# Letting the products of two heads take turns in the scan of an RWKV-7 layer

## The chip, the cores and the metric

The kernel runs on one core of a Trainium2 chip. The metric is the device time of one execution in microseconds (us). The kernel before takes 3988.88 us, the median of three runs (3987.24 to 3991.28). Products of matrices run on TensorE (PE in the profile; its loads of the stationary operand are listed as PEld), everything elementwise on VectorE (DVE), ScalarE (ACT) and GpSimd (POOL); SyncE (SP) and others start DMAs.

## The reference, cut to what matters

One encoder layer for 1024 tokens of 1024 numbers: a combined projection, a branch with forgetting attention, a branch with RWKV-7 time mixing (8 heads of 64), a gated merge, and a block of product-key experts. The change lies in the RWKV-7 branch, whose reference is a loop over the tokens:

```python
def frame_step(state, inp):
    r_t, w_t, k_t, v_t, kk_t, a_t = inp
    sa = jnp.einsum('bhij,bhj->bhi', state, -kk_t)
    state = (state * w_t[:, :, None, :] + sa[..., None] * (kk_t * a_t)[:, :, None, :]
             + v_t[..., None] * k_t[:, :, None, :])
    return state, jnp.einsum('bhij,bhj->bhi', state, r_t)
```

Each head carries a state of 64 x 64; every token decays it, corrects it and reads one row of output from it. All is float32.

## The kernel before, in words

`body` takes the tokens in two halves of 512. A half goes through `fox` (attention), `rwkv_half`, `merge_half` and `queries`; after the second half comes a long phase for the experts (`dense_block`), from about 2070 us to the end, in which PE is busy nearly all the time.

`rwkv_half` treats the eight heads in four groups `ct` of two heads `e`. The two heads of a group share the 128 partitions: `rows[0]` is partitions 0 to 63, `rows[1]` 64 to 127. `unit(ct)` computes one group in chunks of 64 tokens; a half has NC = 8 chunks `c`. It first prepares, for all chunks at once, the matrices that each chunk needs: masked products `M`, transposed operands `BK` and `AV`, a triangular inverse built up in six levels (`Tm`, `Vm`, products of 64 x 64 blocks in PSUM tiles named `s`), and from them `At` (a tile named `Tm`), which carries a head's state over one chunk, and `Q` (a tile named `x`), which reads the outputs.

Then comes the scan (lines 1020 to 1034), the only part that goes chunk by chunk. A step has eight products, four for each head:

- BK: `pss[r] = BK[:, e, c] x AV[:, e, c]` (line 1026), over all 128 partitions with 64 output rows: the profile writes its place on the array as 128*64, and its names as `s<-AV,BK`.
- At: `pss[r] += At[r, c] x sigma[r]` (line 1027), over the head's own 64 partitions, 64*64, `s<-sigma,Tm`. `sigma` is the state.
- M: `py[r, c] = AV x M` (line 1031), 128*64, `s<-M,AV`.
- Q: `py[r, c] += sigma x Q` (line 1032), 64*64, `s<-x,sigma`.

Head 0 writes partitions 0 to 63 of the PSUM tile, head 1 partitions 64 to 127. Between At and M a copy (line 1028) brings `pss` back to SBUF as the next state; DVE makes it in even steps, ACT in odd ones, and there are two places for the state, taken in turn. The next step's At waits for that copy; M and Q of the same step still read the old state. In the profile every float32 product is two PE instructions (x2).

All products go through the helper `mm` (line 262), so they all carry line 263. `mm` also ticks a background (`g.B`): the work for the experts (top-k, gathers of expert rows by POOL, reduces by DVE, line 1403) is issued piece by piece between the products, by an account of estimated product times, and stands between the kernel's own instructions on DVE and POOL. It has something to do only from the second half on, once the first half's scores are known. After each step `wait(WT[7])` lets a filler issue about 1 us of gate projections (`pj` products of 512 columns, lines 324 to 334), as long as there are some left for this group: in the first three groups they fill the places after the first and the second step of a scan, in the fourth those after the first four steps. The steps behind them are bare. PE takes its instructions in the order in which they are written (`manual_schedule`).

Of the kernel before, what the change touches and what calls it, by code (L numbers as in the profile page):

```python
# [261 lines left out]
def mm(g, o, l, r, start, stop_):  # L262
    g.pe.matmul(o, l, r, start=start, stop=stop_)  # L263
    n = 1
    for d in r.shape[1:]:
        n *= d
    us = max(n, 256) / 2400.0 if r.dtype == F32R else max(4 * n, 256) / 2400.0
    g.V.tick(us)
    if not g.V.busy:
        g.B.tick(us)  # L270
# [470 lines left out]
def rwkv_half(g, hf, X, kt):  # L741
# [3 lines left out]
    rows = (slice(0, 64), slice(64, 128))  # L745
# [8 lines left out]
    with ExitStack() as fx:  # L754
# [164 lines left out]
        def unit(ct):  # L919
# [3 lines left out]
            def wait(us):  # L923
                F.fill(WAIT * us)
# [64 lines left out]
            for u in range(0, NC, 8):  # L989
# [3 lines left out]
                for c in range(n8):  # L993
                    for e in range(2):
                        r = rows[e]
                        mm(g, pw[r, c, :], Vm[r, u + c, :], AV[r, e:3:2 - e, u + c, :], True, True)
                act.copy(W_[:, us], pw[:, :, 0:64])
                for e in range(2):
                    r = rows[e]
# [3 lines left out]
            for e, c in items:  # L1003
                r = rows[e]
# [9 lines left out]
            for e, c in items:  # L1014
                r = rows[e]
# [5 lines left out]
            for c in range(NC):  # L1021
                par = c % 2
                pss = psS.tile([128, 64], F32, name="s")
                for e in range(2):
                    r = rows[e]
                    mm(g, pss[r, :], BK[:, e, c, :], AV[:, e, c, :], True, False)
                    mm(g, pss[r, :], At[r, c, :], g.sigma[r, ct, par, :], False, True)
                (act.copy if c % 2 or SM & 64 else dve.tensor_copy)(g.sigma[:, ct, 1 - par, :], pss)
                for e in range(2):
                    r = rows[e]  # L1030
                    mm(g, py[r, c, :], AV[:, e, c, :], M[:, e, c, 0:64], True, False)
                    mm(g, py[r, c, :], g.sigma[r, ct, par, :], Q[r, c, :], False, True)
                wait(WT[7])
            act.copy(yr[:, ct, :], fl(py))
# [13 lines left out]
        for ct in range(4):  # L1048
            F.add(bonus(ct))
            if ct < 3:  # L1050
                F.add(elem(ct + 1), f"e{ct + 1}")
            gates(NG[1 + ct])
            unit(ct)
            if ct < 3:
                F.drain(f"e{ct + 1}")
# [785 lines left out]
```

## Time and profile before

| | |
|---|---|
| median of three runs | 3988.88 us |
| profiled execution | 3954.7 us |
| its span | 3952.9 us |
| PE busy | 3367.2 us (85%), 20656 instructions |
| DVE busy | 2310.8 us (58%) |
| POOL busy | 2341.8 us (59%) |
| ACT busy | 1243.7 us (31%) |
| mean clock granted to TensorE | 0.897 of full speed |

The span is that of one execution, taken by the hardware profiler. A row of a timeline gives start, duration, engine, line, operation, output<-inputs by the program's names, for a product its place on the array (rows*columns) and the moving operand's shape, and in brackets the idle time before it with what ended it. PE is pipelined and the ends of its instructions are modelled: the pace is read from the starts. A table of stretches gives each engine's busy time, and the clock that TensorE was granted as a share of full speed.

### The profile page before, as it was taken

What the parts mean: (1) busy time and instruction counts of PE and PEld (TensorE: products, weight loads), DVE (VectorE), ACT (ScalarE), POOL (GpSimd) and SP (SyncE); (2) the same over time, 40 slices, a digit from 0 to 9 for tenths busy, and PEclk for the clock granted to TensorE, in tenths of its full rate; (3) what the DMA queues carried; (4) which work ended last, traced back from release to release, by engine and by line L of the source; (5) the groups of instructions that cost most, each with busy time, mean ns of one, the idle gap of its engine ahead of it and who ended that gap; (6) DMA issues with size and microseconds to landing.
All of it is one profiled execution on the core that took longest, in us unless ns stands there. A gap on an engine that the chain in (4) does not pass through costs nothing. (4 is left out here: it accounts for less than half of the span.)

```text
span 3952.9 us, 55417 instructions
## 1 busy us (share of the span) xinstructions
PE 3367.2 (85%) x20656; PEld 2429.7 (61%) x20656; DVE 2310.8 (58%) x4773; ACT 1243.7 (31%) x2522; POOL 2341.8 (59%) x1848
## 2 busy tenths in 40 slices
PE   7999999989987877877837676699998899999998
PEld 5577676775555655656713333477776677776676
DVE  3133423448889887899637576366665576733334
ACT  3342212333333111122214343233333333333333
POOL 2031114435666546667647667688887788777872
PEclk9898898998988777888968778799999899999999
DMA  4121114447777666877768789999998999999993
GB/s 134 43 91 36 36 63 138 168 150 243 259 256 260 213 213 223 292 252 262 278 250 269 263 289 301 322 362 367 375 349 319 374 377 387 376 367 406 403 407 128
DMA packets 376575, 1018.03 MB, mean 258 GB/s; under 512 B 108273, under 2 KB 124913, under 8 KB 376049
## 3 DMA queue, kind: packets, MB, share of 16 engines
q0 software_dynamic: 184320, 671.17, 46.5%
q1 hardware_dynamic: 179872, 322.54, 23.9%
q10 hardware_dynamic: 12112, 20.78, 1.4%
q8 instruction: 162, 2.65, 0.3%
q14 instruction: 109, 0.88, 0.1%
HBM read 960.03 MB, written 54.33 MB: 257 GB/s over the span
## 5 line engine op out<-in xcount | busy, mean ns | idle before, releaser
L1398 POOL DMA_INDIRECT g<-u,eidx x640 | 779.0, 1217 | 436.5 <-DVE hh L1403 154.6
L1403 DVE CUSTOM_DVE_ANT_0 g<-g,ext 128x1024 f32<-128x1024 f32 x640 | 879.5, 1382 | 230.3 <-DMA g<-u,eidx 228.7
L281 POOL TENSOR_TENSOR wl<-wraw,wh 128x1024 fp32r<-128x1024 f32 x131 | 322.9, 2465 | 562.4 <-ACT wh L280 513.1
L1675 POOL DMA_INDIRECT vr<-v,ve x454 | 488.6, 1076 | 130.3 <-issue 104.1
L263 PE MATMUL pg<-vr,win 128*32 128x512 f32 x1816 | 307.8, 645 | 115.6 <-DMA vr<-v,ve 115.3
L263 PE MATMUL b<-xh,uh 128*128 128x384 f32 x1024 | 353.7, 345 | 52.2 <-DVE C L1561 29.6
L263 PE MATMUL b<-xh,ul 128*128 128x384 f32 x1024 | 357.4, 349 | 19.1 <-POOL ul L281 19.1
L263 PE MATMUL b<-xl,uh 128*128 128x384 f32 x1024 | 351.9, 344 | 0.0
L263 PE MATMUL v<-vl,ch 128*128 128x512 f32 x768 | 310.1, 404 | 22.7 <-POOL vl L281 22.6
L263 PE MATMUL pj<-xh,wh 128*128 128x512 f32 x624 | 292.0, 468 | 22.3 <-DVE ql L546 8.5
L280 ACT CAST wh<-wraw 128x1024 fp32r<-128x1024 f32 x150 | 157.2, 1048 | 486.3 <-PE pj L263 264.3
L263 PE MATMUL v<-vh,cl 128*128 128x512 f32 x768 | 305.3, 398 | 0.0
L263 PE MATMUL v<-vh,ch 128*128 128x512 f32 x768 | 304.7, 397 | 0.0
L280 ACT CAST uh<-uraw 128x512 fp32r<-128x512 f32 x256 | 158.7, 620 | 399.4 <-PE b L263 359.0
L263 PE MATMUL pj<-xh,wl 128*128 128x512 f32 x624 | 262.0, 420 | 6.4 <-POOL wl L281 3.7
L263 PE MATMUL pj<-xl,wh 128*128 128x512 f32 x624 | 263.9, 423 | 1.9 <-DVE xl L281 1.9
L1675 POOL DMA_INDIRECT C<-v,ve x186 | 196.6, 1057 | 105.3 <-issue 39.4
L263 PEld LDWEIGHTS b<-xh,uh 128*128 128x128 f32 x1024 | 196.7, 192 | 66.5 <-DVE C L1561 34.3
L263 PEld LDWEIGHTS b<-xh,ul 128*128 128x128 f32 x1024 | 196.6, 192 | 56.6 <-issue 32.7
L281 POOL TENSOR_TENSOR ul<-uraw,uh 128x512 fp32r<-128x512 f32 x128 | 170.6, 1333 | 92.8 <-ACT uh L280 66.7
L281 DVE TENSOR_TENSOR vl<-vraw,vh 128x512 fp32r<-128x512 f32 x128 | 122.8, 960 | 171.4 <-ACT vh L280 164.7
L263 PEld LDWEIGHTS pg<-vr,win 128*32 128x32 f32 x1816 | 52.3, 112 | 275.2 <-DMA vr<-v,ve 191.4
(352 smaller groups left out, 6897.9 us busy)
## 6 DMA issues: line engine op xcount, KB each, us to landing
wraw<-w SPq DMA_DIRECT2D x150, 512.0 KB, 3.5
uraw<-ut SPq DMA_DIRECT2D x128, 512.0 KB, 6.9
vraw<-vt SPq DMA_DIRECT2D x128, 512.0 KB, 6.7
cd<-S SPq DMA_DIRECT2D x30, 512.0 KB, 15.6
C<-cd SPq DMA_DIRECT2D x80, 192.0 KB, 6.1
g<-u,eidx POOLq DMA_INDIRECT x640, 6.1
gtd<-tmp ACTq DMA_DIRECT2D x32, 256.0 KB, 3.1
g<-gtd SPq DMA_DIRECT2D x32, 256.0 KB, 3.3
```

The source lines that it names most:

```text
L263: g.pe.matmul(o, l, r, start=start, stop=stop_)
L280: g.act.copy(hi, src)
L281: (lo_eng or g.dve).tensor_sub(lo, src, hi.bitcast(F32))
L1398: pool.indirect_dma_start(out=gg, out_offset=None, in_=A["u"], in_offset=bass.IndirectOffsetOnAxis(ap=idx[:, s_:s_ + 1], axis=0))
L1403: dve.tensor_tensor_reduce(out=gg, in0=gg, in1=xt, scale=1.0, scalar=0.0, op0=OP.mult, op1=OP.add, accum_out=hh[:, k:k + 1])
L1675: g.pool.indirect_dma_start(out=place, out_offset=None, in_=g.A["v"], in_offset=bass.IndirectOffsetOnAxis(ap=self.meta[i][1][:, t:t + 1], ...
```

## The change

The two loops over the heads, each with two products in its body, become four loops with one product each. What is multiplied, added and copied stays the same; only the order of the eight products of a step differs. The wait of the first At product for the state now stands behind both BK products.

```diff
             for c in range(NC):
                 par = c % 2
                 pss = psS.tile([128, 64], F32, name="s")
-                for e in range(2):
-                    r = rows[e]
+
+                for e, r in enumerate(rows):
                     mm(g, pss[r, :], BK[:, e, c, :], AV[:, e, c, :], True, False)
+                for r in rows:
                     mm(g, pss[r, :], At[r, c, :], g.sigma[r, ct, par, :], False, True)
                 (act.copy if c % 2 or SM & 64 else dve.tensor_copy)(g.sigma[:, ct, 1 - par, :], pss)
-                for e in range(2):
-                    r = rows[e]
+                for e, r in enumerate(rows):
                     mm(g, py[r, c, :], AV[:, e, c, :], M[:, e, c, 0:64], True, False)
+                for r in rows:
                     mm(g, py[r, c, :], g.sigma[r, ct, par, :], Q[r, c, :], False, True)
                 wait(WT[7])
```

PE's order at the start of the first scan, before the change: the first step, between the projection that precedes it and the one that fills behind it. The tile s_2412 is `pss` of this step, s_2411 is `py`, Tm_2380 is `At`, x_2406 is `Q`.

```order
L263 MATMUL pj_2323<-xh_84,wl_2218 128x512
L263 MATMUL s_2412<-AV_1788,BK_1787 64x64
L263 MATMUL s_2412<-sigma_138,Tm_2380 64x64
L263 MATMUL s_2412<-AV_1788,BK_1787 64x64
L263 MATMUL s_2412<-sigma_138,Tm_2380 64x64
L263 MATMUL s_2411<-M_1786,AV_1788 64x64
L263 MATMUL s_2411<-x_2406,sigma_138 64x64
L263 MATMUL s_2411<-M_1786,AV_1788 64x64
L263 MATMUL s_2411<-x_2406,sigma_138 64x64
L263 MATMUL pj_2323<-xh_84,wh_2217 128x512
```

The same place after the change (x2 here: the product of head 0, then that of head 1).

```order
L263 MATMUL pj_2323<-xh_84,wl_2218 128x512
L263 MATMUL s_2412<-AV_1788,BK_1787 64x64 x2
L263 MATMUL s_2412<-sigma_138,Tm_2380 64x64 x2
L263 MATMUL s_2411<-M_1786,AV_1788 64x64 x2
L263 MATMUL s_2411<-x_2406,sigma_138 64x64 x2
L263 MATMUL pj_2323<-xh_84,wh_2217 128x512
```

Each kind of product now stands twice in a row, once for each head, and the filling projection stands where it stood. Further on in the same scan, where no projections stand between the steps, before the change:

```order
L263 MATMUL s_2441<-AV_1788,BK_1787 64x64
L263 MATMUL s_2441<-sigma_138,Tm_2380 64x64
L263 MATMUL s_2441<-AV_1788,BK_1787 64x64
L263 MATMUL s_2441<-sigma_138,Tm_2380 64x64
L263 MATMUL s_2411<-M_1786,AV_1788 64x64
L263 MATMUL s_2411<-x_2406,sigma_138 64x64
L263 MATMUL s_2411<-M_1786,AV_1788 64x64
L263 MATMUL s_2411<-x_2406,sigma_138 64x64
L263 MATMUL s_2454<-AV_1788,BK_1787 64x64
```

And after it:

```order
L263 MATMUL s_2441<-AV_1788,BK_1787 64x64 x2
L263 MATMUL s_2441<-sigma_138,Tm_2380 64x64 x2
L263 MATMUL s_2411<-M_1786,AV_1788 64x64 x2
L263 MATMUL s_2411<-x_2406,sigma_138 64x64 x2
L263 MATMUL s_2454<-AV_1788,BK_1787 64x64 x2
```

The last Q product of a step is followed at once by the next step's two BK products, and the copy of the state has those, M and Q to run beside. On DVE, ACT, POOL and SP no instruction changes its place.

## The prediction

> **What bounds the kernel now.** I read the page first (TensorE, PE in the rows, is busy for 85% of the span), then the stretches of the eight scans, then the timeline inside one of them. The profiled execution took 3954.7 us, its span and 1.8 us around it; the three timed runs have a median of 3988.88 us. I work out a saving on the profiled execution and take it from that median. A measurement of this kernel tells about 0.2%, 8 us, from no change.
>
> The stretches of the eight scans (two halves of four groups), from the first product of a scan to the end of its last step. Columns: stretch, its us, then busy us and instructions of PE, PEld, DVE, ACT, POOL, then the granted clock, DMA share and GB/s.
>
> ```profile
> 344.19:367.16 22.97, 22.97 (x138) 16.32 (x137) 1.41 (x5) 2.39 (x6) 2.34 (x1) 0.76 0.11 36
> 426.87:450.28 23.41, 23.41 (x139) 16.60 (x138) 1.41 (x5) 2.39 (x6) 2.34 (x1) 0.74 0.10 34
> 509.47:533.23 23.76, 23.76 (x139) 16.85 (x138) 1.41 (x5) 2.39 (x6) 2.34 (x1) 0.72 0.10 34
> 587.68:611.28 23.60, 23.60 (x148) 16.64 (x147) 2.52 (x6) 2.39 (x6) 0.58 (x1) 0.87 0.33 112
> 1314.81:1345.01 30.20, 27.70 (x140) 19.17 (x139) 14.29 (x53) 2.39 (x6) 12.76 (x11) 0.62 0.60 202
> 1425.15:1457.80 32.65, 28.29 (x138) 19.61 (x137) 18.71 (x45) 4.45 (x8) 14.71 (x13) 0.59 0.63 206
> 1541.02:1575.23 34.21, 28.28 (x140) 19.62 (x139) 17.03 (x44) 2.39 (x6) 16.07 (x12) 0.59 0.64 214
> 1653.02:1679.59 26.57, 25.12 (x148) 17.51 (x147) 18.02 (x54) 2.39 (x6) 15.38 (x13) 0.82 0.84 287
> sum 217.37, PE 203.13 PEld 142.32 DVE 74.80 ACT 21.18 POOL 66.54; mean PE 25.39 PEld 17.79 DVE 9.35 ACT 2.65 POOL 8.32
> ```
>
> The scans take 217 us, 5.5% of the span, and in the first half nothing but PE works in them: DVE is busy 1.4 us of 23. The clock granted is 0.59 to 0.87 there. Now the inside of one scan, in which one step of the loop over c has no projection work between; each row is one product (two instructions, x2).
>
> ```profile
> 352.84 0.33 PE L263 MATMUL s<-AV,BK 128*64 128x64 f32 x2
> 353.10 0.32 PE L263 MATMUL s<-sigma,Tm 64*64 64x64 f32 x2
> 353.36 0.33 PE L263 MATMUL s<-AV,BK 128*64 128x64 f32 x2
> 353.61 0.33 PE L263 MATMUL s<-sigma,Tm 64*64 64x64 f32 x2
> 353.87 0.33 PE L263 MATMUL s<-M,AV 128*64 128x64 f32 x2
> 354.03 0.21 ACT L1028 COPY sigma<-s 128x64 f32<-128x64 f32 x1 [1.78 <-PE s L263]
> ...
> 354.89 0.33 PE L263 MATMUL s<-AV,BK 128*64 128x64 f32 x2
> ...
> 357.48 0.47 PE L263 MATMUL s<-AV,BK 128*64 128x64 f32 x2
> ...
> 360.71 0.47 PE L263 MATMUL s<-AV,BK 128*64 128x64 f32 x2
> ```
>
> A product starts every 0.26 us, whatever stands beside it, and a step of eight takes 354.89 - 352.84 = 2.05 us; later in the same scan, 360.71 - 357.48 = 3.23 us, the same step at the halved clock. The product itself cannot need 0.26 us, as other places show, with the same element type and both heads' partition halves taking turns:
>
> ```profile
> 341.29 1.15 PE L263 MATMUL s<-BK,x 64*64 64x64 f32 x32
> 342.27 1.10 PE L263 MATMUL s<-M,x 64*64 64x64 f32 x32
> 343.30 0.50 PE L263 MATMUL pj<-xh,wh 128*128 128x512 f32 x1
> 343.63 0.39 PE L263 MATMUL pj<-xl,wh 128*128 128x512 f32 x1
> 343.86 0.40 PE L263 MATMUL pj<-xh,wl 128*128 128x512 f32 x1
> 344.19 0.33 PE L263 MATMUL s<-AV,BK 128*64 128x64 f32 x2
> ...
> 2593.68 1.92 PE L263 MATMUL pg<-vr,win 128*32 128x512 f32 x16
> 2595.54 0.45 PE L263 MATMUL b<-xh,ul 128*128 128x384 f32 x1
> ```
>
> Sixteen 64*64 products start within 342.27 - 341.29 = 0.98 us: 0.06 us each, a quarter of the scan's 0.26. What differs is that those sixteen all have one shape, 64 rows by 64 columns of the array, while in the scan each product has another shape than the one before it (128*64, 64*64, 128*64, ...). It is not only that neighbours share a place: the second and third rows of the scan step lie on different columns (head 0's 64*64 corner, then head 1's 128*64 half), and are as far apart as the rest. The Trainium skill says so too ("TensorEngine Tiling (Array Packing)", Key Properties): a change of the tiling mode, not merely of the tile, drains TensorE; by that rule the scan drains eight times a step, and the trace agrees, 0.26 against 0.06 us.
>
> **The change, part by part.** It makes a step BK, BK, At, At, M, M, Q, Q: four changes of shape instead of eight. Nothing is added or removed, and on DVE, ACT, POOL and SP every instruction stands where it stood; the first 64*64 product's wait for sigma moves behind one more product.
>
> *One step.* Each pair now has one shape on two places. What the second product of a pair costs is bounded by 0.06 us (an alternating one, above) and by nearly nothing, if it runs wholly beside the first, as a pair of the sixteen does; so a pair takes 0.26 to 0.32 us. For the 128*64 pair no row exists, since all 128 rows of the array serve both; the nearest is pg, four column strips of 128*32 fed by different data: 16 instructions of 512 columns in 2595.54 - 2593.68 = 1.86 us, where 16 in line at the 0.23 us between two pj rows would take 3.7. Column strips do run side by side, so I take 0.26 for both kinds, and 0.51 (no overlap) as the far end for the 128*64 pair. A step then takes 4 x 0.26 = 1.04 us instead of 2.05.
>
> *Does sigma's chain take over?* In the step shown, the copy starts 354.03 - 353.61 = 0.42 us after the second At product starts and takes 0.21. With both At products starting together, sigma is there 0.63 us after them, and they are due again after 1.04: 0.4 us to spare. M, Q and the next BK (3 x 0.26 = 0.78 us) cover the copy. If that cover went, a step would be some 0.65 us anyway, so the chain does not bind.
>
> *First half.* PE is never idle in these four scans. A projection step between two steps (three pj with its entry) takes 344.19 - 343.30 = 0.89 us, a second one behind it 0.70. The first three scans hold three (0.89 + 1.59 = 2.5 us), the fourth six in four places (5.0). So after the change: 3 x (8.3 + 2.5) + 8.3 + 5.0 = 45.7 us, if the clock stays up; before, 22.97 + 23.41 + 23.76 + 23.60 = 93.7. Saved 48 us, 20 of it from steps at the halved clock.
>
> *The clock.* It was halved after some 5 us of bare steps; a bare stretch of six will last 6.2 us with twice the products in the time, so the clock either holds or drops near its end. Dropping costs about 1 us a scan; holding also frees what follows:
>
> ```profile
> 367.16 2.08 PE L263 MATMUL pm<-arv,bk 64*128 64x128 f32 x16
> ...
> 371.89 0.63 PE L263 MATMUL pj<-xh,wl 128*128 128x512 f32 x1
> 372.32 0.63 PE L263 MATMUL pj<-xh,wh 128*128 128x512 f32 x1
> ...
> 375.71 1.16 PE L263 MATMUL pm<-arv,bk 64*128 64x128 f32 x16
> ```
>
> The first pm after the scan takes 2.08 us instead of 1.16, and pj come every 0.43 instead of 0.23 us: some 2.5 us behind each of four scans, 10 in all. Between -4 and +10 I take +4.
>
> *Second half.* Here DVE carries the experts' reduces and the top-k, and outside the scans PE waits for it. What can be gained is the time in which DVE waits for PE:
>
> ```profile
> DVE sigma L1028 <- PE s L263: 47.4, 11, 7.1
> DVE g L1403 <- DMA g<-u,eidx: 10.7, 15, 2.5
> DVE M L937 <- PE pm L263: 9.8, 3, 3.6
> ```
>
> (waits of DVE from 1310 to 1680 us: us in total, times, longest). And DVE between two of its copies of sigma, the second bare pair of the fifth scan:
>
> ```profile
> 1333.82 0.23 DVE L1028 COPY sigma<-s 128x64 f32<-128x64 f32 x1 [3.09 <-PE s L263]
> ...
> 1334.48 1.21 DVE L1403 CUSTOM_DVE_ANT_0 g<-g,ext 128x1024 f32<-128x1024 f32 x1
> 1335.62 0.08 DVE L1403 DVE_READ_ACCUMULATOR2_ANT hh<- 128x1 f32 x1
> 1340.27 0.23 DVE L1028 COPY sigma<-s 128x64 f32<-128x64 f32 x1 [4.57 <-PE s L263]
> ```
>
> DVE works 1335.70 - 1333.82 = 1.9 us and then waits 4.57. Two steps will take 2.1 us, so the work just fits and some 0.3 us of waiting is left. The wait before the first bare copy (7.1 us, behind a filled step at low clock) shrinks only by about 2. Left over I estimate 5 us for each of three scans and 2 for the last, with 3 at pm: 20 of 47.4 + 9.8 = 57. That frees 37, and DVE, the slower engine around these scans, hands it on; gathers that now come late may take 3 of it back: 34 us, between 0 and all 57.
>
> *Sum.* 48 + 4 + 34 = 86 us: profiled 3954.7 - 86 = 3869, and the median 3988.88 - 86 = **3903 us**. What comes later moves up by it: the order on every engine is the same, and the last phase is a chain of PE.
>
> **Rivals.**
>
> 1. *DVE swallows the second half.* For it: DVE's 1.9 us between copies against 2.1 us; a gather that lands late eats that. Against: only 10.7 us of DVE waits for gathers now, longest 2.5. Saved 48 + 3 = 51: 3938 us.
> 2. *128*64 pairs do not overlap.* No row has this shape in turns; pg speaks against. A step is 2 x 0.26 + 4 x 0.26 = 1.56 us, half the saving, 24 + 18 = 42: 3947 us.
> 3. *64*64 pairs do not overlap,* as both heads write one PSUM tile from different row halves. Only the 128*64 pairs gain: 42 us again, 3947. The sixteen products at 0.06 us do just that (both halves of one tile) and speak against it. This is the Trainium skill's rule against the change ("TensorEngine Tiling (Array Packing)", Gotcha 1: PSUM Pressure): different row tiles cannot access one PSUM bank at the same time; by these rows the trace does not bear it out.
> 4. *No change:* each product drains by itself, with its accumulation, and pairs keep 0.26 each: 3989 us. The alternating rows are single products, not accumulating ones; that is all that speaks for it.
> 5. *Slower:* in the second half a copy of sigma stands behind a reduce whose gather has lost its lead, and PE waits for it. The price of one:
>
> ```profile
> L1398 POOL DMA_INDIRECT g<-u,eidx x640 | 779.0, 1217 | 436.5 <-DVE hh L1403 154.6
> L1403 DVE CUSTOM_DVE_ANT_0 g<-g,ext 128x1024 f32<-128x1024 f32 x640 | 879.5, 1382 | 230.3 <-DMA g<-u,eidx 228.7
> ...
> g<-u,eidx POOLq DMA_INDIRECT x640, 6.1
> ```
>
> Issue 1.2, landing 6.1, reduce 1.4: 8.7 us, 16 times, 139 us. The four scans last 30.20 + 32.65 + 34.21 + 26.57 = 123.6 us now, 14 of it with PE idle (PE is busy 109.4); at the new pace they would last 46 + 14 + 139 = 199, 75 more, less the first half's 52: 23 slower, 4012 us. It decides from (52 + 64) / 16 = 7.2 us a copy; the gathers are issued three reduces ahead, so I hold it unlikely.
>
> **Chances.** Forecast 0.68, rival 1 0.14, rival 2 0.08, rival 3 0.04, rival 4 0.03, rival 5 0.03. The forecast's own range goes from 48 + 10 + 57 = 115 us saved (the clock holds, DVE waits for nothing in the second half), 3874, to 40 - 4 + 18 = 54 saved (pairs of 0.32, which cost 32 steps 0.24 us each; the clock drops; half of the second half's gain), 3935. Eight in ten need most of that and rival 1: 3876 to 3942. Faster by over 0.2%: 0.68 + 0.14 + 0.08 + 0.04 = 0.94; within 0.2%: 0.03; slower: 0.03.
>
> **What would show it.** In the profile after: equal products in pairs, a bare step of 1.04 us at clock 1.00 (1.56 means that one kind does not overlap, 2.05 neither); first-half scans of 10.8 us; copies of sigma with DVE waiting under 1 us before them in the second half, the row DVE sigma <- PE s near 15 instead of 47; the waits for g<-u no longer than now. The prediction is wrong if bare steps stay above 1.5 us, or if the first half shrinks by 48 us and the second not at all.

## The result, and the profile after

The changed kernel takes 3880.14 us, the median of six runs (3873.97 to 3887.82), beside 3985.46 us of before (the median of six runs, three of them those above): 105 us less, a ratio of 0.9741 with a 95% interval from 0.9723 to 0.9759. It was forecast at 3903 us, with a range from 3876 to 3942; the time lies inside, near the fast end.

The page's first line, and the stretches of the eight scans after the change (columns as in the prediction):

```profile
span 3878.1 us, 55417 instructions
```

```profile
342.25:353.16 10.91, 10.91 (x138) 7.82 (x137) 1.42 (x5) 2.39 (x6) 2.35 (x1) 1.00 0.22 75
410.18:421.09 10.91, 10.91 (x138) 7.81 (x137) 1.42 (x5) 2.39 (x6) 2.35 (x1) 1.00 0.20 74
478.08:488.99 10.91, 10.91 (x138) 7.81 (x137) 1.42 (x5) 2.39 (x6) 2.35 (x1) 1.00 0.20 73
541.71:555.10 13.39, 13.39 (x147) 9.35 (x146) 2.63 (x6) 2.39 (x6) 0.58 (x1) 1.00 0.47 156
1271.26:1289.20 17.94, 14.51 (x140) 9.93 (x139) 12.92 (x43) 2.22 (x6) 8.55 (x9) 0.71 0.77 262
1373.26:1394.70 21.44, 14.54 (x138) 9.89 (x137) 18.68 (x42) 4.46 (x8) 12.44 (x11) 0.72 0.81 273
1477.64:1502.80 25.16, 17.55 (x138) 11.92 (x137) 17.47 (x44) 2.39 (x6) 16.54 (x13) 0.58 0.86 299
1585.09:1609.70 24.61, 21.71 (x148) 14.39 (x147) 17.19 (x54) 2.39 (x6) 14.61 (x11) 0.55 0.79 278
sum 135.27, PE 114.43 PEld 78.92 DVE 73.14 ACT 21.02 POOL 59.77; mean PE 14.30 PEld 9.87 DVE 9.14 ACT 2.63 POOL 7.47
```

The scans fell from 217.4 to 135.3 us. In the first half they lost half their time and the clock stayed at 1.00 throughout (0.72 to 0.87 before); in the second half they are still twice as long, at a clock of 0.55 to 0.72, with nearly as much DVE work in them as before (66 us against 68). One bare step of the first scan:

```profile
347.91 0.34 PE L263 MATMUL s<-AV,BK 128*64 128x64 f32 x4
...
348.17 0.33 PE L263 MATMUL s<-sigma,Tm 64*64 64x64 f32 x4
...
348.43 0.34 PE L263 MATMUL s<-M,AV 128*64 128x64 f32 x4
...
348.60 0.21 ACT L1029 COPY sigma<-s 128x64 f32<-128x64 f32 x1 [0.29 <-PE s L263]
...
348.70 0.33 PE L263 MATMUL s<-x,sigma 64*64 64x64 f32 x4
...
348.96 0.34 PE L263 MATMUL s<-AV,BK 128*64 128x64 f32 x4
```

A row now holds a pair (x4), and pairs start every 0.26 us, where single products did. A step takes 348.96 - 347.91 = 1.05 us instead of 2.05. What follows the first scan, and the waits of DVE from 1265 to 1612 us (total, times, longest), which answer to 47.4, 10.7 and 9.8 us before (lines 1028 and 1403 of before are 1029 and 1404 here):

```profile
353.17 1.16 PE L263 MATMUL pm<-arv,bk 64*128 64x128 f32 x16
...
355.93 0.39 PE L263 MATMUL pj<-xh,wh 128*128 128x512 f32 x1
356.17 0.39 PE L263 MATMUL pj<-xl,wh 128*128 128x512 f32 x1
```

```profile
DVE sigma L1029 <- PE s L263: 19.4, 10, 4.1
DVE g L1404 <- DMA g<-u,eidx: 8.7, 10, 2.3
...
DVE M L937 <- PE pm L263: 1.2, 1, 1.2
```

The pm stage behind the scan runs at the full clock at once (1.16 us, 2.08 before). DVE waits 28 us less for PE's scan, 9 us less for the pm products, and a little less for gathers.

### The profile page after: what moved, and what is told of

Its sections match the earlier page's. It is cut to its first block, busy times and chain, and to the rows that moved or that the text cites. A ratio compares the mean times of both kernels' runs of the same rounds, so it can differ in the third digit from the quotient of the medians.

```text
span 3878.1 us, 55417 instructions
## 1 busy us (share of the span) xinstructions
PE 3278.8 (85%) x20656; PEld 2368.3 (61%) x20656; DVE 2320.0 (60%) x4773; ACT 1242.7 (32%) x2522; POOL 2347.1 (61%) x1848
## 5 line engine op out<-in xcount | busy, mean ns | idle before, releaser
L1399 POOL DMA_INDIRECT g<-u,eidx x640 | 787.1, 1230 | 421.6 <-DVE hh L1404 142.5
L263 PEld LDWEIGHTS b<-xh,uh 128*128 128x128 f32 x1024 | 195.7, 191 | 67.0 <-DVE C L1562 34.5
```

The source lines that it names most:

```text
L1399: pool.indirect_dma_start(out=gg, out_offset=None, in_=A["u"], in_offset=bass.IndirectOffsetOnAxis(ap=idx[:, s_:s_ + 1], axis=0))
```

## The experiments

The theory: a change of shape on the array drains PE, which costs time at each change of shape, and the changed kernel has half as many of them. The main rival is the change's own description: neighbours must lie on different parts of the array. Beside that stand two questions of size: what limits the second half, and why the two first traces differ by 75 us where the times differ by 105. The diffs of the first, second and fourth experiment are against the changed kernel, that of the third against before.

**Same shape, same place.** Four changes of shape a step as in the changed kernel, but both products of a pair belong to one head. M can move ahead of At because it does not read the state; of the two output products only Q does.

```diff
                 for e, r in enumerate(rows):
                     mm(g, pss[r, :], BK[:, e, c, :], AV[:, e, c, :], True, False)
-                for r in rows:
+                    mm(g, py[r, c, :], AV[:, e, c, :], M[:, e, c, 0:64], True, False)
                     mm(g, pss[r, :], At[r, c, :], g.sigma[r, ct, par, :], False, True)
+                    mm(g, py[r, c, :], g.sigma[r, ct, par, :], Q[r, c, :], False, True)
                 (act.copy if c % 2 or SM & 64 else dve.tensor_copy)(g.sigma[:, ct, 1 - par, :], pss)
-                for e, r in enumerate(rows):
-                    mm(g, py[r, c, :], AV[:, e, c, :], M[:, e, c, 0:64], True, False)
-                for r in rows:
-                    mm(g, py[r, c, :], g.sigma[r, ct, par, :], Q[r, c, :], False, True)
```

Expected: 

> A step's products in the order BK, M, At, Q of head 0, then BK, M, At, Q of head 1: four changes of shape a step, as in the changed kernel, but the two neighbours of one shape lie on the same place of the array. Theory (a change of shape drains): a pair on one place cannot run side by side but costs no drain between, 0.26 and some 0.06 to 0.11 us, so a bare step is 1.3 to 1.45 us and the kernel is 60 to 80 us faster than before. Rival (neighbours must lie on different parts): no gain, bare steps 2.05 us, the same time as before.

Measured: 3898.5 us, ratio to before 0.9777 (0.9735 to 0.9819), some 86 us faster. Half of a bare step in its trace:

```profile
349.24 0.33 PE L263 MATMUL s<-AV,BK 128*64 128x64 f32 x2
349.41 0.28 PE L263 MATMUL s<-M,AV 128*64 128x64 f32 x2
349.62 0.32 PE L263 MATMUL s<-sigma,Tm 64*64 64x64 f32 x2
349.78 0.28 PE L263 MATMUL s<-x,sigma 64*64 64x64 f32 x2
349.99 0.33 PE L263 MATMUL s<-AV,BK 128*64 128x64 f32 x2
```

Behind a product of its own shape, on the very same place, the next one starts 0.16 us later; to the next shape it is 0.21. A pair takes 0.37 us, a step 1.49, where two products of different shape take 0.51: one change of shape less saves 0.14 us. Much of the change's gain is had without two neighbours of one shape on different parts; the rival, which expected none, falls. It came out a little slower a step and faster in all than I had put it. A step saves 0.56 us here where the changed kernel's saves 1.00, yet the kernel saves 86 of its 105 us: in the second half, where DVE shares the path, the stretch of the scans took 338.2 us in this kernel's profile and 338.1 and 334.3 in two of the changed kernel.

**Other places, other shapes.** Six of eight neighbours on different columns, but every one of another shape; for head 1 the two products of a sum change their order.

```diff
                 for e, r in enumerate(rows):
-                    mm(g, pss[r, :], BK[:, e, c, :], AV[:, e, c, :], True, False)
-                for r in rows:
-                    mm(g, pss[r, :], At[r, c, :], g.sigma[r, ct, par, :], False, True)
+                    r1 = rows[1 - e]
+                    mm(g, pss[r, :], BK[:, e, c, :], AV[:, e, c, :], not e, bool(e))
+                    mm(g, pss[r1, :], At[r1, c, :], g.sigma[r1, ct, par, :], not e, bool(e))
+                    mm(g, py[r, c, :], AV[:, e, c, :], M[:, e, c, 0:64], not e, bool(e))
+                    mm(g, py[r1, c, :], g.sigma[r1, ct, par, :], Q[r1, c, :], not e, bool(e))
                 (act.copy if c % 2 or SM & 64 else dve.tensor_copy)(g.sigma[:, ct, 1 - par, :], pss)
-                for e, r in enumerate(rows):
-                    mm(g, py[r, c, :], AV[:, e, c, :], M[:, e, c, 0:64], True, False)
-                for r in rows:
-                    mm(g, py[r, c, :], g.sigma[r, ct, par, :], Q[r, c, :], False, True)
```

Expected: 

> A step's products in the order BK of head 0, At of head 1, M of head 0, Q of head 1, then BK of head 1, At of head 0, M of head 1, Q of head 0 (for head 1 At starts the sum and BK ends it, and so for Q and M): six of eight neighbours lie on different columns of the array, but every neighbour has another shape. Theory (a change of shape drains): eight drains a step, bare steps of 2.05 us, the same time as before within 0.3%. Rival (neighbours must lie on different parts): bare steps of 1.0 to 1.3 us, 70 us or more faster than before.

Measured: 3981.79 us, ratio 0.9981 (0.9956 to 1.0006): no change. Its trace has before's pace:

```profile
357.89 0.33 PE L263 MATMUL s<-AV,BK 128*64 128x64 f32 x2
358.15 0.32 PE L263 MATMUL s<-sigma,Tm 64*64 64x64 f32 x2
358.41 0.33 PE L263 MATMUL s<-M,AV 128*64 128x64 f32 x2
...
359.95 0.33 PE L263 MATMUL s<-AV,BK 128*64 128x64 f32 x2
```

A step is 359.95 - 357.89 = 2.06 us. Different places alone bring nothing. It also answers another rival, that a product waits for the one before it because both add into the same place of PSUM: here no product adds into the place that the one before it wrote, and the pace stays. With the experiment above, this settles what the cost hangs on: the shape first, and among equal shapes the place. Of the 1.00 us that the change takes off a step, 0.56 come with the shapes alone (2.05 to 1.49) and 0.44 with parting the places (1.49 to 1.05; 0.37 us a pair on one place, 0.26 on two). All shapes of this scan have 64 columns and differ in their rows; what a change in the columns costs was not tried.

**One part alone.** BK and At in pairs, the outputs as before: six changes of shape.

```diff
-                for e in range(2):
-                    r = rows[e]
+                for e, r in enumerate(rows):
                     mm(g, pss[r, :], BK[:, e, c, :], AV[:, e, c, :], True, False)
+                for r in rows:
                     mm(g, pss[r, :], At[r, c, :], g.sigma[r, ct, par, :], False, True)
```

Expected: 

> One part of the change alone: BK, BK, At, At in pairs, the outputs still M, Q, M, Q: six changes of shape a step. Theory (a change of shape drains, each product or pair of one shape costs 0.26 us between two drains): 2 x 0.26 + 4 x 0.26 = 1.56 to 1.57 us a bare step at full clock, about half of the gain of the whole change, 40 to 60 us faster than before. Rival (the gain comes from taking sigma's wait out of the way, which this part does alone): bare steps of 1.1 us and most of the gain.

Measured: 3931.91 us, ratio 0.9878 (0.9845 to 0.9911), 53 us faster: half of the gain, as the count of changes says. The rival that put the gain down to sigma's wait would have had most of it here, and falls. A step in its trace, singles and pairs side by side:

```profile
347.70 0.34 PE L263 MATMUL s<-AV,BK 128*64 128x64 f32 x4
347.96 0.33 PE L263 MATMUL s<-sigma,Tm 64*64 64x64 f32 x4
348.22 0.33 PE L263 MATMUL s<-M,AV 128*64 128x64 f32 x2
348.48 0.33 PE L263 MATMUL s<-x,sigma 64*64 64x64 f32 x2
...
349.25 0.34 PE L263 MATMUL s<-AV,BK 128*64 128x64 f32 x4
```

A pair costs what a single product costs, 0.26 us; the step is 1.55.

**Two changes a step.** All four 128*64 products first, then all four 64*64.

```diff
                 for e, r in enumerate(rows):
                     mm(g, pss[r, :], BK[:, e, c, :], AV[:, e, c, :], True, False)
+                for e, r in enumerate(rows):
+                    mm(g, py[r, c, :], AV[:, e, c, :], M[:, e, c, 0:64], True, False)
                 for r in rows:
                     mm(g, pss[r, :], At[r, c, :], g.sigma[r, ct, par, :], False, True)
                 (act.copy if c % 2 or SM & 64 else dve.tensor_copy)(g.sigma[:, ct, 1 - par, :], pss)
-                for e, r in enumerate(rows):
-                    mm(g, py[r, c, :], AV[:, e, c, :], M[:, e, c, 0:64], True, False)
                 for r in rows:
                     mm(g, py[r, c, :], g.sigma[r, ct, par, :], Q[r, c, :], False, True)
```

Expected: 

> A step's products in the order BK, BK, M, M, At, At, copy, Q, Q: two changes of shape a step instead of four. Theory (a change of shape drains): two drains of 0.15 us a step go as well; by PE alone a step is 2 x (0.26 + 0.12) = 0.76 us, and the chain of the state (At products, copy, next At) about 0.65 to 0.75 us, so bare steps are 0.75 to 0.85 us and the kernel is 8 to 20 us faster than the changed one. Rival (the chain or DVE binds already): bare steps stay at 1.05 us and the time is that of the changed kernel.

Measured: 3858.1 us, ratio to before 0.9661 (0.9618 to 0.9704): 22 us under the changed kernel by the medians, a little more than expected; the two were measured in different sets of runs, but the changed kernel's interval (0.9723 to 0.9759) lies wholly above. It is the fastest version of this study. A bare step:

```profile
350.41 0.34 PE L263 MATMUL s<-AV,BK 128*64 128x64 f32 x4
...
350.57 0.29 PE L263 MATMUL s<-M,AV 128*64 128x64 f32 x4
...
350.79 0.33 PE L263 MATMUL s<-sigma,Tm 64*64 64x64 f32 x4
...
350.95 0.28 PE L263 MATMUL s<-x,sigma 64*64 64x64 f32 x4
...
351.17 0.34 PE L263 MATMUL s<-AV,BK 128*64 128x64 f32 x4
```

0.76 us from one BK to the next, as worked out. A second pair of the same shape adds 0.12 us to the first, where a change of shape would have made it 0.26: again 0.14 us for one change.

**The state's copies on ACT**, in the changed kernel and in the order with two changes. In both one constant makes ACT copy the state in every step:

```diff
-SM = 45
+SM = 109
```

Expected of the changed kernel with it: 

> The changed kernel with all eight copies of the state of a scan on ACT (before, DVE made those of the even steps). In the changed kernel's second half DVE still waits 19.4 us for PE before its copies, and PE waits 2.6 us for DVE's copies. Theory (DVE limits the second half, so idle time taken from DVE comes out of the time): DVE no longer stands behind PE in the scans, its background runs on through them, and the kernel is 5 to 15 us faster than the changed one, 3865 to 3875 us. Rival (only PE's own pace in the scans counts there): 0 to 3 us, 3877 to 3880 us. In the first half nothing changes, 1.05 us a bare step, unless ACT's other work is in the way.

Measured: 3877.45 us, ratio to before 0.9744 (0.9717 to 0.9771), the same as the changed kernel. Its stretch of the second half's scans, and the one that follows up to the first product of the experts' one-hot matrices:

```profile
1269.30:1585.30 316.00, 240.99 (x2962) 183.26 (x2963) 291.11 (x679) 67.36 (x119) 204.64 (x155) 0.82 0.79 267
1585.30:1976.60 391.30, 265.48 (x1139) 197.79 (x1139) 296.75 (x672) 96.27 (x150) 261.83 (x178) 0.82 0.76 259
```

```profile
DVE g L1404 <- DMA g<-u,eidx: 17.4, 14, 3.3
```

The first is 18 to 22 us shorter than in two profiles of the changed kernel (338.1 and 334.3); some 6 us come back in the next stretch (385.5 in the changed kernel), and DVE's waits for gathers doubled, to 17.4 us. That speaks for DVE's place behind PE holding the scans up, but does not show it: the profiled execution was the quickest of the six (3863.7 us, 14 under their median), and the medians of the timed runs show nothing of it. The theory's total failed.

Expected of the order with two changes: 

> The order with two changes of shape a step (BK, BK, M, M, At, At, copy, Q, Q) and all copies of the state on ACT. With DVE's copies that order took 0.76 us a bare step, and some steps of the second half 0.9 to 2.2 us behind DVE. Theory (DVE limits the second half): 5 to 15 us faster than that order with DVE's copies, 3843 to 3853 us. Rival: the same within 3 us, 3855 to 3861 us; or slower, because in steps of 0.76 us ACT's casts of weights (1.05 us) stand ahead of a copy and the bare steps grow in the first half.

Measured: 3865.91 us, ratio 0.9706 (0.9681 to 0.9731). That is not faster than with DVE's copies (0.9661); the intervals overlap, so slower isn't certain. In its profile the second half's scans took 315.3 us where DVE's copies had 328.2, so the stretch is shorter in this pair of profiles too, and again the time is not; where it goes is not shown. Bare steps of the first half stayed at 0.76 us save one of 1.23, so they do not explain it. Copies on ACT are not worth having.

**Before and after once more**, for the spread of single executions.

Expected of the first repetition of before: 

> The kernel before, once more, for a second profile. The first profile of before (span 3952.9 us) was 31 us under the median of its timed runs (3985 us), while the profile of the changed kernel agrees with its timed runs, so the traces show 75 us and the times 105 us. Theory (the clock): the granted clock of stretches outside the scans differs from execution to execution, and the first profile had a good one (1.00 from 1066 to 1116 us, where the changed kernel was granted 0.90); a second profile comes out nearer to 3985 and grants less there, 0.90 to 0.95, while the scans have bare steps of 2.05 and 3.23 us as before. Rival (the profile): a profiled execution of before is always quicker than a timed one; then it is 3953 again, with 1.00 there. Time against before: the same.

Measured: 3982.6 us, ratio 0.9986 (0.996 to 1.0012); span of its profile 3969.6 us. The theory was right that the first profile was a quick one, and wrong in the place it named: from 1066 to 1116 us the clock is 1.00 here as well. The rival, that a profiled execution of before is always that quick, falls with this span and the next.

Expected of another: 

> The kernel before, a third profile, for the spread of its stretches. Theory: first stretch 267 us within 1 us, the second half's scans between 364 and 376 us, the rest of the span between 3320 and 3345 us as in the first two profiles (3321.5 and 3328.7) and beyond. Rival: the rest is as short as the changed kernel's, 3327 us or less, in all.

Measured: 4001.14 us in one run, span 3999.4 us. The first stretch came out as expected; the second half's scans took 383.0 us, longer than the 364 to 376 expected, and the rest of the span, 3348.6, lay a little beyond its range.

Expected of the changed kernel: 

> The changed kernel once more, for a second profile. In the first one the stretch from the first scan's start to the fourth's end was 54 us shorter than in two profiles of before (212.7 against 266.8 and 267.4 us), that of the second half's scans 26 and 35 us shorter (338.2 against 364.5 and 373.5). Theory (the gain is in the scans, and what lies between the sums of the traces and the 105 us of the timed runs is the spread of single executions): the first stretch repeats within 1 us, the second within 10 us, and the rest of the span differs from the first profile by up to 20 us either way. Rival (something outside the scans became faster too): the rest is shorter than in every profile of before, 3272 us or less.

Measured: 3881.27 us, ratio to before 0.9748 (0.972 to 0.9777), span 3873.8 us. All three parts came out within what was expected. The stretches from the first scan to the end of the fourth, and from the fifth to the end of the eighth, in the first profile of before,

```profile
344.20:611.00 266.80, 257.46 (x2963) 194.13 (x2963) 84.42 (x144) 53.70 (x93) 37.45 (x21) 0.88 0.14 49
...
1314.80:1679.30 364.50, 293.10 (x2963) 219.03 (x2963) 291.97 (x707) 64.32 (x103) 207.79 (x159) 0.77 0.71 238
```

and in the first profile of the changed kernel:

```profile
342.30:555.00 212.70, 203.33 (x2964) 156.50 (x2963) 84.25 (x144) 53.70 (x93) 37.44 (x21) 0.98 0.17 58
...
1271.30:1609.40 338.10, 252.50 (x2962) 191.78 (x2963) 299.61 (x704) 64.45 (x103) 203.68 (x157) 0.78 0.75 255
```

The other two profiles of before have 267.5 and 373.5 us, and 267.8 and 383.0; the second of the changed kernel has 212.7 and 334.3. The first half's stretch repeats within 1 us; the second half's, where PE and DVE wait for each other, ranges over 18 us in before. With three profiles of before and two of the changed kernel, in us:

| | before, mean | after, mean | saved |
|---|---|---|---|
| first half's scans and what lies between | 267.4 | 212.7 | 54.7 |
| second half's | 373.7 | 336.2 | 37.5 |
| the rest of the span | 3332.9 (3321.6 to 3348.6) | 3327.0 | 6 |
| span | 3974.0 | 3876.0 | 98 |

The rest of the changed kernel is longer than in the first profile of before (3321.6), so the rival, something outside the scans that became faster, is not borne out; the 6 us lie within the spread. The three spans of before rise as the mean granted clock falls (3952.9 at 0.897, 3969.6 at 0.895, 3999.4 at 0.889); that goes together, and which causes which was not tried.

## Why the prediction was right, and where its sizes were off

- *What drains PE.* Right in that the change of shape costs the time, and now shown by an order that keeps the places apart and gains nothing, one that keeps them together and gains 86 us, and by the steps of 2.05, 1.55, 1.05 and 0.76 us with eight, six, four and two changes. With the places left as they are, one change costs 0.14 us. The Trainium skill's sentence on it ("TensorEngine Tiling (Array Packing)", Key Properties: a change of mode drains, a change of tile does not) agrees with these runs in both halves.
- *One step.* Forecast 1.04 us, measured 1.05. The 128*64 pair, for which no row existed, overlaps as column strips do (0.26 us), and the 64*64 pair overlaps though both heads write one PSUM tile: rivals 2, 3 and 4 fall. The Trainium skill's rule that different row tiles cannot access one PSUM bank at the same time ("TensorEngine Tiling (Array Packing)", Gotcha 1: PSUM Pressure) made no cost here that the trace shows: the 64*64 pair takes 0.26 us, as a single product does.
- *Sigma's chain.* Right: it does not bind at 1.05 us. At 0.76 us (two changes a step) it still did not in the first half: the bare steps there are 0.76 us each.
- *First half.* 48 us forecast for the scans; 93.7 - (3 x 10.91 + 13.39) = 47.6 measured.
- *The clock.* Taken at +4 us between -4 and +10. It held at 1.00 in the scans, and the stretch shrank by 54.7 - 47.6 = 7 us more than they did. The prediction's time of some 5 us of bare steps does not decide it: with steps of 1.49 us the clock held through 9 us of them.
- *Second half.* 34 us forecast. In the first two profiles the scans themselves went from 123.6 to 89.2 us, 34.5, but the stretch around them only from 364.5 to 338.1, 26.4: 8 us came back between the scans. Over all profiles the stretch shrank by 37.5 on the average, and by 26 to 49 from one pair of profiles to another, so it is in part luck that 34 came so near. The mechanism is right: DVE's wait for PE's scan was 47.4, 51.2 and 59.4 us in the three profiles of before, 19.4 and 15.8 in the two after, where I had put 15. Something like rival 5 came once: in the sixth scan a reduce took 3.93 us instead of 1.2, the state's copy stood behind it, and PE waited for the copy. What made the reduce long is not shown.

```profile
1388.88 0.23 DVE L1029 COPY sigma<-s 128x64 f32<-128x64 f32 x1 [0.41 <-PE s L263]
...
1389.21 3.93 DVE L1404 CUSTOM_DVE_ANT_0 g<-g,ext 128x1024 f32<-128x1024 f32 x1
...
1393.21 0.21 DVE L1029 COPY sigma<-s 128x64 f32<-128x64 f32 x1
...
1393.48 0.48 PE L263 MATMUL s<-sigma,Tm 64*64 64x64 f32 x4 [1.75 <-DVE sigma L1029]
```

- *The sum* is the term that was mis-sized: 86 us against 98 in the profiles and 105 in the times. Of the 12, 3 belong to the clock, 3 or 4 to the second half and 6 to the rest of the span. The last I had put at nothing, and the first profile of before, the quickest of three, hid how far that rest and the second half vary. The 7 us between profiles and times lie within that spread and stay open.

## What to carry to other kernels

Small products that alternate between shapes on the array pay at every change (0.14 us here, at the full clock): order them by shape first, then let equal shapes alternate between places, and look at starts, not at PE's busy share, which stood at 100% in the scans of the first half before and after. A gain on PE counts in full where PE alone works, and where another engine shares the path look for the idle time that this engine still has: in this kernel the gain came out of it. One profile of a kernel whose engines wait for each other is one draw: take two or three before a difference of 20 us is explained.

## What the runs showed of the hardware that was not expected

Two kernels whose paces hardly differ were granted different clocks. With steps of 1.49 us (equal shapes on one place) the first scan kept the full clock to its end, through 9 us of bare steps (349.24 to 358.20). With steps of 1.55 us (one part alone) the first scan kept it for four bare steps and the second for three; then the clock fell (in the second scan a step of 1.55 us, then 2.08 and 2.43). The first 13.1 us of the first scan in the one kernel, and most of the bare steps of the first and of the second scan in the other; the clock is the third number from the end:

```profile
343.70:356.80 13.10, 13.10 (x123) 10.25 (x123) 1.29 (x5) 2.18 (x5) 2.35 (x1) 1.00 0.18 62
```

```profile
347.70:357.00 9.30, 9.30 (x89) 6.82 (x88) 0.67 (x3) 1.88 (x4) 2.35 (x1) 0.84 0.25 86
426.60:434.80 8.20, 8.20 (x65) 5.89 (x65) 0.45 (x2) 0.43 (x2) 0.64 (x1) 0.66 0.28 96
```

The two kernels issue the same products at nearly the same rate, and PE's busy share is 100% in all these stretches, so neither tells when the clock falls; what decides it was not tried. Nor does a clock of half the speed double a step of the scan: in before, where 0.50 was granted, it took 3.23 us instead of 2.05, 1.57 times as long.
